# The output projection of a hybrid decoder block: seven block products for eight, and the low parts of its weights made by DMA

## The chip, the cores and the metric

The kernel runs on one core of one Trainium2 chip. The metric is the device time of one execution in microseconds; of the kernel before there are three timed runs and one execution under the profiler. Times in the text that name no run are microseconds from the start of the profiled span.

## The reference

One layer of a hybrid block on x of 2048 tokens by 1024 channels, all in float32. An input projection feeds a pooling mixer (512 channels) and a gated DeltaNet (4 heads of 128), their results are put side by side, and an output projection with a residual and a last norm ends it:

```python
n = rms_norm(h, norm_w[layer])
proj = jnp.einsum('bsd,de->bse', n, w_in[layer])
...
y_pool = pool_mixer(pu, pz, pool_w[layer], pool_scale[layer])
y_dn = deltanet_mixer(q, k, v, dz, b, a, conv_w[layer], a_log[layer],
                      dt_bias[layer], dn_norm_w[layer])
y = jnp.concatenate([y_pool, y_dn], axis=-1)
h = h + jnp.einsum('bse,ed->bsd', y, w_out[layer])
return rms_norm(h, final_norm_w)
```

The change is in the last two lines: y (2048 x 1024) times w_out (1024 x 1024), plus x, then the norm of each row.

## The kernel before

TensorE multiplies in a rounded 32-bit format (fp32r). To keep float32's precision each operand is written as a high part (rounded to fp32r) and a low part (the rest), and each product of two operands is made of three matmuls: high by high, high by low, low by high. All of them are 128x128 weights against 512 columns.

The kernel walks the sequence in two blocks of 1024 tokens, and in each through the input projection (L375 to L377), whose results feed the convolutions, the pooling and the DeltaNet chain of each head. The branches' results go to a DRAM buffer, y_dram, in 16 tiles of 128 tokens (L405, by SP's queue). After the last projection comes the output stage, on which this document turns:

- W_out is held in two halves of 512 columns, nh (high) and nl (low), in the buffers which the normalised input of the last block had (two of each, so the first half can come as soon as the first half block's projections have ended, the second when the last has). load_wo (L838) fetches raw pieces of 512 KB by SP's queue into four buffers of the DeltaNet part, split_wo (L842) copies them to nh on ScalarE (L847) and subtracts for nl on VectorE (L178).
- Each tile of y is loaded into wh by GpSimd's queue (load_y, L858), and its low part made in wl by split_y: ScalarE writes minus the high part (L865) and a DMA from GpSimd's queue adds y to it on the way (L866, accum_op=add: an accumulating DMA). wh and wl have three buffers each, which the weights of the input projection had before.
- out_mm (L868) makes for a tile, a half of the columns and one of eight slices of 128 channels the three matmuls L872, L873 and L874. A tile's half is eight slices, 24 matmuls; in the text a slot is one slice, three matmuls. The stage has 16 tiles, 256 slots, 768 matmuls.
- out_add (L876) adds the residual on VectorE (L881) and sums the squares on ScalarE (L883); out_norm (L885) makes 1/sqrt by 13 small steps on VectorE (L888, L889 and rsqrt, L168 to L175), scales (L895) and stores (L898, SP's queue).

TensorE's order is the order in which the events are traced: at(slot, function) gives each step its slot, and the steps are sorted by it. On the other engines a scheduler sets the order when the kernel is built; each engine and each DMA queue then takes its instructions strictly in that order. Two queues issue the kernel's DMAs: SP's (plain transfers) and GpSimd's (POOL; plain and accumulating).

Of the kernel before, what the change touches and what calls it, by code (L numbers as in the profile page):

```python
# [19 lines left out]
NB = SEQ // TB  # L20
HALF = 512
# [24 lines left out]
    (("dec", 4), ("dec", 4), ("dec", 4), ("kdec", 2)),  # L46
    (("dec", 4), ("kdec", 2), ("kT", 2), ("kT", 2)),
)
WO_TAGS = ("At", "Ai", "Tt", "kT")

E_PU, E_PZ, E_Q, E_K, E_V, E_Z = 0, 4, 8, 12, 16, 20

# [25 lines left out]
def hymba_kernel(  # L78
# [18 lines left out]
    nc = tc.nc  # L97
# [9 lines left out]
    def st(shape, dt, tag, bufs=1):  # L107
        return sp.tile(shape, dt, tag=tag, name=tag, bufs=bufs)
# [68 lines left out]
    def split_lo(eng, lo, full, hi):  # L177
        eng.tensor_tensor(out=lo, in0=full, in1=hi, op=ALU.subtract)  # L178
# [163 lines left out]
    events = []  # L342
# [1 line left out]
    free.update({(t, i): -99 for t in ("kdec", "kT", "qT", "sz") for i in range(2)})  # L344

    def at(slot, fn, *args):
        events.append((slot, len(events), fn, args))

    def load_w(w, et, first):
        w["hi"] = st([P, KT, P], F32R, "wh", 3)  # L350
# [384 lines left out]
    slot = 0  # L735
# [3 lines left out]
    for b in range(NB):  # L739
# [13 lines left out]
        i = 0  # L753
# [79 lines left out]
        for h, res in heads:  # L833
            delta(b, h, res, gt, ends[h], ready)

    wo = {"hi": {}, "lo": {}}
# [5 lines left out]
    def split_wo(i, hf):  # L842
# [4 lines left out]
        nc.scalar.copy(wo["hi"][hf][:, ks], wo["raw", i, hf])  # L847
        split_lo(nc.vector, wo["lo"][hf][:, ks], wo["raw", i, hf], wo["hi"][hf][:, ks])

    def load_fw():  # L850
        wo["fw"] = fw = st([P, D], F32, "v0")
        nc.gpsimd.dma_start(fw, final_w[None, :].to_broadcast([P, D]))

    def load_y(ti, o):
        o["y"] = y_dram[ti]
        o["hi"] = st([P, KT, P], F32R, "wh", 3)
        o["lo"] = st([P, KT, P], F32R, "wl", 3)
        nc.gpsimd.dma_start(o["hi"], o["y"])  # L858

    def load_res(ti, o):  # L860
        o["x"] = xr = st([P, D], F32, "kdec", 2)
        nc.sync.dma_start(xr, x[ti * P : (ti + 1) * P, :])

    def split_y(o):
        nc.scalar.activation(o["lo"], o["hi"].bitcast(F32), AF.Copy, scale=-1.0)  # L865
        nc.gpsimd.dma_start(o["lo"], o["y"], accum_op=ALU.add)  # L866

    def out_mm(o, hf, k):  # L868
        if k == 0:
# [3 lines left out]
        nc.tensor.matmul(ps, o["hi"][:, k], wo["lo"][hf][:, k], start=False, stop=False)  # L873
        nc.tensor.matmul(ps, o["lo"][:, k], wo["hi"][hf][:, k], start=False, stop=(k == KT - 1))  # L874

    def out_add(o, hf):  # L876
        if hf == 0:
            o["h"] = st([P, D], F32, "dec", 4)
            o["s2"] = st([P, 2], F32, "s2o", 2)
        dsl = slice(hf * HALF, (hf + 1) * HALF)  # L880
        nc.vector.tensor_tensor(out=o["h"][:, dsl], in0=o["ps", hf], in1=o["x"][:, dsl], op=ALU.add)  # L881
        junk = st([P, HALF], F32, "acc", 3)
        nc.scalar.activation(junk, o["h"][:, dsl], AF.Square, accum_out=o["s2"][:, hf : hf + 1])  # L883

    def out_norm(ti, o):  # L885
        ht, s2 = o["h"], o["s2"]
        v = st([P, 1], F32, "vo", 2)
        nc.vector.tensor_tensor(out=v, in0=s2[:, 0:1], in1=s2[:, 1:2], op=ALU.add)  # L888
        nc.vector.tensor_scalar(out=v, in0=v, scalar1=1.0 / D, scalar2=EPS, op0=ALU.mult, op1=ALU.add)  # L889
        r = st([P, 1], F32, "ro", 2)  # L890
        rsqrt(r, v, [P, 1])
        step = HALF if ti == SEQ // P - 1 else D
        for o0 in range(0, D, step):
            cs = slice(o0, o0 + step)
            nc.vector.scalar_tensor_tensor(  # L895
                out=ht[:, cs], in0=ht[:, cs], scalar=r[:, 0:1], in1=wo["fw"][:, cs], op0=ALU.mult, op1=ALU.mult
            )
            nc.sync.dma_start(out[ti * P : (ti + 1) * P, cs], ht[:, cs])  # L898
# [7 lines left out]
    order = []  # L906
    for i in range(0, SEQ // P, 2):
        if i == 0:
            order += [(i, 0), (i + 1, 0), (i, 1), (i + 1, 1)]
        else:  # L910
            order += [(i, 0), (i, 1), (i + 1, 0), (i + 1, 1)]
    for ti, hf in order:
        o = outs[ti]
        if hf == 0:
            at(slot - 30, load_y, ti, o)
            at(slot - 20, load_res, ti, o)
            at(slot - 20, split_y, o)
        for k in range(KT):
            at(slot + k, out_mm, o, hf, k)
        slot += KT  # L920
        at(slot, out_add, o, hf)
        if hf == 1:
            at(slot + 1, out_norm, ti, o)

    with tc.manual_schedule(engines={mybir.EngineType.PE}):
        for _, _, fn, args in sorted(events, key=lambda e: e[:2]):
            fn(*args)


def layout(inputs):  # L930
# [42 lines left out]
```

## Time and profile before

| what | value |
|---|---|
| three timed runs | 1006.75, 1006.88, 1007.75 us (median 1006.88) |
| the profiled execution | 1006.09 us, of it the span 1004.4 us |
| mean granted TensorE clock | 0.994 |
| busy in the window 900 to 950 us (all output stage) | TensorE 50.00 of 50.00, VectorE 22.11, ScalarE 11.84 |
| the same window's DMA share and rate | 0.71, 199 GB/s |
| first matmul of the output stage | 820.5 us |

A row of a timeline gives the start, the duration, the engine, the line and operation, and in brackets how long the engine stood idle before it and what ended that. Matmuls overlap: each is shown with 0.39 us, and they start 0.2267 us apart. A row of a table by windows gives the window, its length, the busy time and count of each engine (PE, weight loads, VectorE, ScalarE, GpSimd), the granted clock, the DMA share (mean busy share of the 16 DMA engines) and GB/s. For a DMA instruction the duration is that of its issue, not of the transfer.

### The profile page before, as it was taken

How to read it: one execution, taken by the hardware profiler on the slowest of the kernel's cores; microseconds unless marked ns; L12 is line 12 of the kernel's file. 1: busy time of each engine (PE TensorE's matmuls, PEld its weight loads, DVE VectorE, ACT ScalarE, POOL GpSimd, SP SyncE). 2: the span in 40 equal slices, each digit the busy share in tenths (PEclk: the TensorE clock that was granted, in tenths of full speed). 3: DMA queues.
4: the chain of work that ended last, by engine and by line, in shares of the span. 5: the costliest groups of instructions: out<-in, count | busy, mean ns of one | idle time of the engine just before them, and what ended most of it. 6: DMA issues, size and time to landing. Idle time of an engine off the chain costs nothing.

```text
span 1004.4 us, 14802 instructions
## 1 busy us (share of the span) xinstructions
PE 950.2 (95%) x5252; PEld 757.1 (75%) x5252; DVE 652.3 (65%) x2032; ACT 485.4 (48%) x1205; POOL 147.6 (15%) x200
## 2 busy tenths in 40 slices
PE   4989999989999999999899999999999999999996
PEld 3667777778777787767677777777778778888885
DVE  6676978668588355957886866858835483443343
ACT  7357665565564435516855455556443332222211
POOL 2214200101000014104410010101001101111100
PEclk9999999999999999999999999999999999999999
DMA  7431333332424346424242242242444576777761
GB/s 252 90 84 43 75 78 58 77 82 45 112 64 113 78 105 163 101 58 106 57 91 42 62 92 60 48 89 63 103 108 106 151 195 178 193 206 195 185 185 63
DMA packets 49434, 106.90 MB, mean 106 GB/s; under 512 B 4688, under 2 KB 22352, under 8 KB 49360
## 3 DMA queue, kind: packets, MB, share of 16 engines
q0 software_dynamic: 18000, 65.54, 30.4%
q1 hardware_dynamic: 31360, 40.41, 12.1%
q8 instruction: 41, 0.67, 0.3%
q14 instruction: 33, 0.27, 0.1%
HBM read 89.16 MB, written 16.78 MB: 105 GB/s over the span
## 4 chain that ended last, share of the span: by engine, by line
PE 56%; DVE 6%; issue 6%; DMA 4%; ACT 4%; POOL 0%; DVEq 0%; ACTq 0%; POOLq 0%
PE ps L375 10%; PE ps L377 9%; PE ps L376 9%; PE pso L874 6%; PE pso L873 6%; PE pso L872 6%; DMA wh<-in_w_in_dram 3%; PE ch L631 1%; PE tp L465 1%; DVE Ai L511 1%; PE qp L532 1%; PE ch L653 1%; PE ob L641 1%; PE ch L647 1%; PE ob L657 1%
## 5 line engine op out<-in xcount | busy, mean ns | idle before, releaser
L375 PE MATMUL ps<-nh,wh 128*128 128x512 f32 x768 | 335.6, 437 | 10.6 <-ACT nh L193 10.6
L377 PE MATMUL ps<-nh,wl 128*128 128x512 f32 x768 | 303.0, 395 | 1.8 <-DMA wl<-in_w_in_dram 1.8
L376 PE MATMUL ps<-nl,wh 128*128 128x512 f32 x768 | 302.3, 394 | 2.3 <-DVE nl L194 2.3
L375 PEld LDWEIGHTS ps<-nh,wh 128*128 128x128 f32 x768 | 145.9, 190 | 36.9 <-ACT nh L193 11.2
L377 PEld LDWEIGHTS ps<-nh,wl 128*128 128x128 f32 x768 | 145.0, 189 | 34.9 <-DMA wl<-in_w_in_dram 2.7
L376 PEld LDWEIGHTS ps<-nl,wh 128*128 128x128 f32 x768 | 146.1, 190 | 27.7 <-DVE nl L194 4.4
L389 DVE SCALAR_TENSOR_TENSOR acc<-u,cw,acc 128x512 f32<-128x512 f32 x144 | 112.5, 781 | 10.7 <-ACT acc L387 9.1
L872 PE MATMUL pso<-nh,wh 128*128 128x512 f32 x256 | 100.0, 391 | 0.0
L874 PE MATMUL pso<-nh,wl 128*128 128x512 f32 x256 | 99.7, 389 | 0.2 <-DMA wl<-y_dram 0.2
L873 PE MATMUL pso<-nl,wh 128*128 128x512 f32 x256 | 99.6, 389 | 0.0
L358 POOL DMA_DIRECT2D wh<-in_w_in_dram x46 | 26.6, 579 | 388.1 <-PE ps L377 375.0
L881 DVE TENSOR_TENSOR dec<-pso,kdec 128x512 f32<-128x512 f32 x32 | 22.1, 691 | 80.1 <-PE pso L874 80.1
L384 DVE TENSOR_TENSOR u<-ps,rb 128x512 f32<-128x512 f32 x48 | 33.1, 689 | 57.5 <-PE ps L377 57.3
L366 ACT ACTIVATE wl<-wh 128x1024 fp32r<-128x1024 f32 x46 | 48.8, 1061 | 44.0 <-DMA wh<-in_w_in_dram 35.2
L367 POOL DMA_DIRECT2D wl<-in_w_in_dram x46 | 39.7, 863 | 184.9 <-ACT wl L366 93.4
L883 ACT ACTIVATE acc<-dec 128x512 f32<-128x512 f32 x32 | 20.1, 629 | 85.3 <-DVE dec L881 85.3
L387 ACT ACTIVATE acc<-u,cw 128x512 f32<-128x512 f32 x48 | 34.6, 721 | 54.5 <-DVE u L384 52.4
L548 DVE TENSOR_TENSOR tmp<-Ai,X 128x60 f32<-128x60 f32 (+24 forms) x248 | 53.5, 216 | 4.0
L874 PEld LDWEIGHTS pso<-nh,wl 128*128 128x128 f32 x256 | 48.1, 188 | 10.6 <-DMA wl<-y_dram 0.6
L872 PEld LDWEIGHTS pso<-nh,wh 128*128 128x128 f32 x256 | 48.1, 188 | 10.2 <-ACT nh L847 0.2
L873 PEld LDWEIGHTS pso<-nl,wh 128*128 128x128 f32 x256 | 48.1, 188 | 10.0 <-issue 0.2
L554 DVE TENSOR_TENSOR X<-X,tmp 128x60 f32<-128x60 f32 (+24 forms) x248 | 52.5, 212 | 4.5
(214 smaller groups left out, 1511.4 us busy)
## 6 DMA issues: line engine op xcount, KB each, us to landing
wh<-in_w_in_dram POOLq DMA_DIRECT2D x46, 512.0 KB, 3.8
wl<-in_w_in_dram POOLq DMA_DIRECT2D x46, 512.0 KB, 5.6
y_dram<-yt SPq DMA_DIRECT2D x32, 256.0 KB, 3.1
kdec<-in_x_dram SPq DMA_DIRECT2D x16, 512.0 KB, 4.5
wh<-y_dram POOLq DMA_DIRECT2D x16, 512.0 KB, 4.0
wl<-y_dram POOLq DMA_DIRECT2D x16, 512.0 KB, 6.4
out_dram<-dec SPq DMA_DIRECT2D x15, 512.0 KB, 2.7
dec<-in_xT_dram SPq DMA_DIRECT2D x7, 512.0 KB, 7.8
```

The source lines that it names most:

```text
L366: nc.scalar.activation(w["lo"], w["hi"].bitcast(F32), AF.Copy, scale=-1.0)
L367: nc.gpsimd.dma_start(w["lo"], w_in[et], accum_op=ALU.add)
L375: nc.tensor.matmul(ps, w["hi"][:, k], nh[:, k], start=(k == 0), stop=False)
L376: nc.tensor.matmul(ps, w["hi"][:, k], nl[:, k], start=False, stop=False)
L377: nc.tensor.matmul(ps, w["lo"][:, k], nh[:, k], start=False, stop=(k == KT - 1))
L387: nc.scalar.activation(acc, ub[:, HALO:], AF.Copy, scale=cw[:, ci, CONV - 1 : CONV])
L389: nc.vector.scalar_tensor_tensor(out=acc, in0=ub[:, h0 + j : h0 + j + HALF], scalar=cw[:, ci, j : j + 1], in1=acc, op0=ALU.mult, op1=ALU.add,)
L548: nc.vector.tensor_tensor(out=tmp[:, 0:n, 0:w], in0=Ai[:, j, j + 1 : BS].unsqueeze(1).to_broadcast([P, n, w]), in1=X[:, 0:n, j : j + 1].to ...
L554: nc.vector.tensor_tensor(out=X[:, 0:n, j + 1 : BS], in0=X[:, 0:n, j + 1 : BS], in1=tmp[:, 0:n, 0:w], op=ALU.subtract)
L872: nc.tensor.matmul(ps, o["hi"][:, k], wo["hi"][hf][:, k], start=(k == 0), stop=False)
L873: nc.tensor.matmul(ps, o["hi"][:, k], wo["lo"][hf][:, k], start=False, stop=False)
L874: nc.tensor.matmul(ps, o["lo"][:, k], wo["hi"][hf][:, k], start=False, stop=(k == KT - 1))
```

## The change

Tiles 0 to 3 are computed as before, though the right half of the columns (hf=1) goes ahead of the left. The other twelve are taken in six pairs. For a pair, the two tiles are the two block rows of a 2x2 block matrix A (columns: the two halves of the 1024 channels) and W_out is the 2x2 block matrix B. The four block results take eight block products, which a Strassen scheme (Winograd's form) makes of seven with sums of blocks. Each block product is four slots, so that a pair has 28 slots, 84 matmuls, in place of 96:

```diff
+    PRODUCTS = (
+        ("A", "A11", "B11", True),
+        ("C", "S1", "T1", True),
+        ("B", "A12", "B21", True),
+        ("A", "S2", "T2", False),
+        ("C", "S4", "B22", False),
+        ("D", "A22", "T4", True),
+        ("A", "S3", "T3", False),
+    )
```

A, B, C, D are PSUM banks. Bank A is read after its first product, accumulated on, read again, accumulated on again. The sums of W_out's blocks, T1 to T4, are made once, in the time of tiles 0 to 3, from pieces of W_out that SP's queue loads again as float32 (t_load). Each T is split into high (ScalarE copy) and low (ScalarE minus the high, then an accumulating DMA whose source is an SBUF tile):

```diff
+    def lower(lo, hi, src):
+        nc.scalar.activation(lo, hi.bitcast(F32), AF.Copy, scale=-1.0)
+        nc.gpsimd.dma_start(lo, src, accum_op=ALU.add)
...
     def load_wo(i, hf):
-        wo["raw", i, hf] = wr = st([P, 2, HALF], F32, *((t := WO_TAGS[(4 * hf + i) % len(WO_TAGS)]), 2 if t == "kT" else 1))
-        nc.sync.dma_start(wr, w_out[:, 2 * i : 2 * i + 2, hf * HALF : (hf + 1) * HALF])
...
+        nc.gpsimd.dma_start(wo["hi"][hf][:, 2 * i : 2 * i + 2], wo_src(i, hf))
+
+    def split_wo(i, hf):
         ks = slice(2 * i, 2 * i + 2)
-        nc.scalar.copy(wo["hi"][hf][:, ks], wo["raw", i, hf])
-        split_lo(nc.vector, wo["lo"][hf][:, ks], wo["raw", i, hf], wo["hi"][hf][:, ks])
+        lower(wo["lo"][hf][:, ks], wo["hi"][hf][:, ks], wo_src(i, hf))
+
+    def t_load(k, w):
+        w["bd"] = bd = st([P, 2, HALF], F32, "yr1", 2)
+        nc.sync.dma_start(bd, w_out[:, k : KT : NP, half(1)])
+        w["a"], w["c"] = st([P, HALF], F32, "u", 3), st([P, HALF], F32, "acc" if k == 3 else "rb", 3)
+        nc.sync.dma_start(w["a"], w_out[:, k, half(0)])
+        nc.sync.dma_start(w["c"], w_out[:, k + NP, half(0)])
+
+    def t_sums(k, w):
+        a, b, c, d = w["a"], w["bd"][:, 0], w["c"], w["bd"][:, 1]
+        minus = lambda o, x0, x1: nc.vector.tensor_tensor(out=o, in0=x0, in1=x1, op=ALU.subtract)
...
+    def t_split(k, w, name):
...
+        nc.scalar.copy(hi, w[name])
+        lower(lo, hi, w[name])
```

A pair's y comes by SP's queue as float32 (pair_load) and is summed and split on VectorE and ScalarE (pair_a, pair_b, pair_c: 5 casts of 512 columns and one of 1024 on ScalarE, 4 sums, 5 subtractions of 512 and one of 1024 on VectorE). The residual comes in by an accumulating DMA onto a copy of a PSUM bank, four of 256 KB for each pair:

```diff
+    def pair_seed(q, bank, o, ti, hf):
+        if "h" not in o:
+            o["h"] = st([P, D], F32, "dec", 4)
+        nc.scalar.copy(o["h"][:, half(hf)], q[bank])
+        nc.gpsimd.dma_start(o["h"][:, half(hf)], x[ti * P : (ti + 1) * P, half(hf)], accum_op=ALU.add)
```

Each pair's two norms are made together, with the 13 steps for both tiles at once; only those of the last pair apart, the second after the last add. Most steps of the stage on the other engines are "paced": they get an order dependency, without a semaphore, on the matmul traced last before them, so that the scheduler does not put them ahead of it:

```diff
+            for ins in new:
+                if held and ins.engine != mybir.EngineType.PE:
+                    tc.add_manual_dep(ins, last.name, no_sync, reason="paced")
...
-            at(slot - 22 + 16 * hf + 0.1 * i, load_wo, i, hf)
-            at(slot - 14 + 15 * hf + 3 * i, split_wo, i, hf)
+            paced(slot - 16 + 15.5 * hf + 0.1 * i, load_wo, i, 1 - hf)
+            paced(slot - 12 + 15 * hf + 2 * i, split_wo, i, 1 - hf)
+    for k in range(NP):
+        w = {}
+        paced(slot + 6 + 6 * k, t_load, k, w)
+        ts = slot + 14 + 6 * k
+        paced(ts, t_sums, k, w)
+        paced(ts + 0.1, t_split, k, w, "T2")
+        paced(ts + 0.2, t_split, k, w, "T1")
+        paced(ts + 0.3, t_split, k, w, "T3")
+        paced(slot + 45 + 2 * k, t_split, k, w, "T4")
...
+        paced(slot - 32, pair_load, t, q)
+        paced(slot - 14, pair_a, q)
+        paced(slot - 10, pair_b, q)
+        paced(slot - 3, pair_c, q)
...
+        paced(done[0], pair_seed, q, "A", o1, t, 0)
+        paced(done[1], pair_seed, q, "C", o2, t + 1, 1)
+        paced(done[3], pair_seed, q, "A", o1, t, 1)
+        paced(done[5], pair_seed, q, "D", o2, t + 1, 0)
```

Nothing ahead of the output stage changes on TensorE. GpSimd's queue at the start of the stage, before (wh and wl are tiles of y from y_dram, high and low; v0 is the final norm's weight):

```order
L858 DMA wh_8147<-y_dram_93 128x1024
L367 DMA wl_7980<-in_w_in_dram 128x1024
L866 DMA wl_8148<-y_dram_93 128x1024
L852 DMA v0_8280<-in_final_norm_w_dram 128x1024
L858 DMA wh_8212<-y_dram_93 128x1024
L866 DMA wl_8213<-y_dram_93 128x1024
L858 DMA wh_8353<-y_dram_93 128x1024
L866 DMA wl_8354<-y_dram_93 128x1024
```

The same place now (nh and nl are the halves of W_out, high and low; line 864 is the accumulating DMA of lower, for y and W_out alike):

```order
L912 DMA wh_8147<-y_dram_93 128x1024
L387 DMA wl_7980<-in_w_in_dram 128x1024
L907 DMA v0_8276<-in_final_norm_w_dram 128x1024
L864 DMA wl_8148<-y_dram_93 128x1024
L873 DMA nh_8239<-in_w_out_dram 128x2x512 x4
L864 DMA nl_8240<-in_w_out_dram 128x2x512
L912 DMA wh_8210<-y_dram_93 128x1024
L864 DMA nl_8240<-in_w_out_dram 128x2x512 x3
L873 DMA nh_8324<-in_w_out_dram 128x2x512 x4
L864 DMA wl_8211<-y_dram_93 128x1024
L912 DMA wh_8344<-y_dram_93 128x1024
L864 DMA nl_8325<-in_w_out_dram 128x2x512 x4
```

Between the tiles of y stand now sixteen transfers of W_out, eight of them accumulating; the low part of the second tile (wl_8211) stands behind the second half's four high parts.

Further down the same queue, where before only wh and wl of the next tiles follow in turn (tiles 3 and 4, and the high part of tile 5), before:

```order
L858 DMA wh_8431<-y_dram_93 128x1024
L866 DMA wl_8432<-y_dram_93 128x1024
L858 DMA wh_8532<-y_dram_93 128x1024
L866 DMA wl_8533<-y_dram_93 128x1024
L858 DMA wh_8616<-y_dram_93 128x1024
```

and now (qT, Tt and sz hold the low parts of T1, T3 and T2; wh_8395 and wl_8396 are tile 3):

```order
L864 DMA qT_8430<-u_8367 128x512
L864 DMA wl_8345<-y_dram_93 128x1024
L864 DMA Tt_8435<-yr1_8365 128x512
L864 DMA sz_8425<-yr1_8365 128x512
L864 DMA qT_8430<-u_8403 128x512
L864 DMA Tt_8435<-yr1_8401 128x512
L864 DMA sz_8425<-yr1_8401 128x512
L912 DMA wh_8395<-y_dram_93 128x1024
L864 DMA wl_8396<-y_dram_93 128x1024
```

Five accumulating transfers of 256 KB stand between the low part of tile 2 and tile 3, a sixth ahead of both.

SP's queue around the start of the stage, before:

```order
L405 DMA y_dram_93<-yt_8174 128x4x128
L840 DMA At_8311<-in_w_out_dram 128x2x512
L840 DMA Ai_8313<-in_w_out_dram 128x2x512
L840 DMA Tt_8315<-in_w_out_dram 128x2x512
L405 DMA y_dram_93<-yt_8262 128x4x128
L405 DMA y_dram_93<-yt_8361 128x4x128
L862 DMA kdec_8403<-in_x_dram 128x1024
```

and now (yr1, u, rb and acc are the pieces of W_out for the T sums, dec the residual):

```order
L425 DMA y_dram_93<-yt_8174 128x4x128
L916 DMA dec_8264<-in_x_dram 128x1024
L425 DMA y_dram_93<-yt_8256 128x4x128
L881 DMA yr1_8365<-in_w_out_dram 128x2x512
L883 DMA u_8367<-in_w_out_dram 128x512
L884 DMA rb_8368<-in_w_out_dram 128x512
L425 DMA y_dram_93<-yt_8354 128x4x128
L881 DMA yr1_8401<-in_w_out_dram 128x2x512
L883 DMA u_8403<-in_w_out_dram 128x512
L884 DMA rb_8404<-in_w_out_dram 128x512
L916 DMA dec_8410<-in_x_dram 128x1024
L883 DMA u_8455<-in_w_out_dram 128x512
```

The loads for the T sums stand on this queue from just before the stage's start on.

More of the change, by code (lines that the diff above doesn't have):

```diff
@@ L885, in out_norm @@
[L885 to L888, printed above, removed]
-        nc.vector.tensor_scalar(out=v, in0=v, scalar1=1.0 / D, scalar2=EPS, op0=ALU.mult, op1=ALU.add)
[L890 to L898, printed above, removed]
+        nc.vector.tensor_tensor(out=o["h"][:, half(hf)], in0=ps, in1=src[:, half(hf)], op=ALU.add)
@@ new lines, in pair_sums, with pair_load, pair_split @@
+    def pair_sums(t):
+        sq = st([P, 2, 2], F32, "s2o", 2)
+        for j in range(2):
+            outs[t + j]["sq"], outs[t + j]["s2"] = sq, sq[:, j]
+    def pair_load(t, q):
+        q["r1"] = st([P, KT, P], F32, "yr1", 2)
+        nc.sync.dma_start(q["r1"], y_dram[t])
+        for name, tag, lo in (("r21", "ps_s", 0), ("r22", "sacc", NP)):
+            q[name] = st([P, NP, P], F32, tag, 2)
+            nc.sync.dma_start(q[name], y_dram[t + 1][:, lo : lo + NP])
+    def pair_split(hi, lo, raw):
+        nc.scalar.copy(hi, raw)
+        split_lo(nc.vector, lo, raw, hi)
@@ new lines, in pair_mm @@
+    def pair_mm(q, bank, a, b, fresh, k):
+        if fresh and k == 0:
+            pool, tag = BANKS[bank]
+            q[bank] = pool.tile([P, HALF], F32, tag=tag, name="ps" + bank)
+        ps = q[bank]
+        (ah, al), (bh, bl) = (t[:, k] for t in q[a]), w_part(b, k)
+        args = dict(skip_group_check=True)
+        nc.tensor.matmul(ps, ah, bh, start=(fresh and k == 0), stop=False, **args)
+        nc.tensor.matmul(ps, ah, bl, start=False, stop=False, **args)
+        nc.tensor.matmul(ps, al, bh, start=False, stop=(k == NP - 1), **args)
@@ L904, in hymba_kernel @@
     at(slot - 10, load_fw)
     outs = [{} for _ in range(SEQ // P)]
[L906 to L912, printed above, removed]
-        o = outs[ti]
[L914 to L917, printed above, removed]
+    for ti, hf in ((0, 1), (1, 1), (0, 0), (1, 0), (2, 1), (3, 1), (2, 0), (3, 0)):
+        o = outs[ti]
+        if hf == 1:
+            paced(slot - 30, load_y, ti, o)
+            paced(slot - 20, load_res, ti, o)
+            paced(slot - 20, split_y, ti, o)
+            if ti % 2 == 0:
+                at(slot, pair_sums, ti)
```

141 lines of the change are left out of this document (119 added, 22 removed).

## The prediction, on record before the changed kernel was run

> **What bounds the kernel now.** I read the page first, for the engines' shares and the slices. They say that TensorE is full to the end and that the DMA engines are busiest in the last fifth:
>
> ```profile
> PE 950.2 (95%) x5252; PEld 757.1 (75%) x5252; DVE 652.3 (65%) x2032; ACT 485.4 (48%) x1205; POOL 147.6 (15%) x200
> DMA  7431333332424346424242242242444576777761
> ```
>
> Then TensorE's waits from 740 us to the end, two in all, 0.9 us together:
>
> ```profile
> PE ps L377 <- DMA wl<-in_w_in_dram: 0.7, 1, 0.7
> PE pso L874 <- DMA wl<-y_dram: 0.2, 1, 0.2
> ```
>
> So the output stage is bound by the number of its matmuls. Their spacing and the stage's ends come from TensorE's timeline (two rows 21 matmuls apart, the last matmul, the first step behind it) and from the group of line 872:
>
> ```profile
> 900.05 0.39 PE L872 MATMUL pso<-nh,wh 128*128 128x512 f32 x1
> ...
> 904.81 0.39 PE L872 MATMUL pso<-nh,wh 128*128 128x512 f32 x1
> ...
> 995.70 0.39 PE L874 MATMUL pso<-nh,wl 128*128 128x512 f32 x1
> 996.13 0.69 DVE L881 TENSOR_TENSOR dec<-pso,kdec 128x512 f32<-128x512 f32 x1 [4.75 <-PE pso L874]
> ```
>
> ```profile
> L872 PE MATMUL pso<-nh,wh x256: 389/389/798, 820.5 to 995.2; 128*128 128x512 f32 x128
> ```
>
> (904.81 - 900.05)/21 = 0.2267 us for a matmul, 0.68 us for a slot. The stage starts at 820.5, its last matmul at 995.7. From the first step behind TensorE (996.13) to the end of the span (1004.4) it is 8.3 us, and the profiled execution's 1006.1 us hold 1.7 us beside the span. The median of the timed runs is 0.8 us above that execution, under the 0.2% (2 us) that a measurement of this kernel can tell from no change; I forecast for the profiled execution and let the median stand at the same place.
>
> **What the seven products save.** The order of the changed kernel shows 84 matmuls for each of six pairs where 96 were: 72 x 0.2267 = 16.3 us, all on TensorE and so all on the path, if TensorE stays fed.
>
> **What a transfer costs.** The change moves W_out's low parts from VectorE to accumulating DMAs. VectorE's subtractions (row of 1.22 us below, eight) hid beside TensorE, which waited for none of them, so removing them gains nothing. The price of the DMAs is in windows in which one transfer ran nearly alone (a fetch of 512 KB issued at 625.14, an accumulate of 512 KB at 630.36), in one that holds the four transfers of a tile (wl, wh, residual, result), and in the kernel's last store:
>
> ```profile
> 625.14 0.56 POOL L358 DMA_DIRECT2D wh<-in_w_in_dram  x1 [12.13 <-PE ps L377]
> 630.36 0.85 POOL L367 DMA_DIRECT2D wl<-in_w_in_dram  x1 [4.66 <-ACT sqj L472]
> ```
>
> ```profile
> 626.00:629.00 3.00, 1.22 (x7) 0.93 (x7) 2.96 (x13) 1.56 (x5) 0.00 (x0) 1.00 0.55 178
> 631.00:636.00 5.00, 5.00 (x31) 4.39 (x30) 4.29 (x20) 2.02 (x9) 0.21 (x1) 1.00 0.67 105
> 855.00:864.00 9.00, 9.00 (x41) 7.46 (x40) 4.29 (x16) 1.97 (x4) 0.68 (x2) 1.00 0.81 235
> ```
>
> ```profile
> q1 hardware_dynamic: 288, 0.52, 14.1%
> ```
>
> The last two columns of a window are DMA share and GB/s. Alone, a fetch keeps all 16 engines for 3 x 0.55 = 1.65 us, an accumulate for 5 x 0.67 = 3.35 us. The last 0.52 MB (queue row of the window 995 to 1005) take 14.1% of 10 us, 1.41. The tile's four take 9 x 0.81 = 7.3 us, so an accumulate among others costs 7.3 - 3 x 1.41 = 3.1. I take 1.4 for a plain unit of 512 KB and 3.1 for an accumulating one, since the change runs them close together as that window does; the lone prices are the upper end. The Trainium skill ("DMA: Bandwidth & Descriptors", "Anatomy of one DMA — SWDGE (gpsimd) path") prices a transfer at about 2.0 us plus bytes over 436 GB/s and sets nothing apart for adding; by that a unit of either kind would move in 1.2 us, an estimate from that page, and the sum below would end at 1002.2, faster. The trace's 3.35 us for a lone accumulate speaks against it.
>
> Transfers of GpSimd's queue finish in its order. Issued 0.56 us apart, the accumulate ends TensorE's wait at 827.61 and the fetch behind it ends ScalarE's at 828.82, 6.2 us after its issue:
>
> ```profile
> 822.08 0.88 POOL L866 DMA_DIRECT2D wl<-y_dram  x1 [6.23 <-ACT wl L865]
> 822.64 0.89 POOL L858 DMA_DIRECT2D wh<-y_dram  x1
> 827.61 0.50 PE L874 MATMUL pso<-nh,wl 128*128 128x512 f32 x1 [0.16 <-DMA wl<-y_dram]
> 828.82 1.06 ACT L865 ACTIVATE wl<-wh 128x1024 fp32r<-128x1024 f32 x1 [2.73 <-DMA wh<-y_dram]
> ```
>
> **The walk through the queue.** W_out's first half can't be fetched before the last block's first half leaves nh. The trace has that moment, where ScalarE's first copy was let go, and the one at which tile 1's buffer came free:
>
> ```profile
> 808.93 1.05 ACT L847 CAST nh<-At 128x1024 fp32r<-128x1024 f32 x1 [8.17 <-PE ps L377]
> 815.30 0.55 POOL L858 DMA_DIRECT2D wh<-y_dram  x1 [12.81 <-PE ps L377]
> ```
>
> First bytes move some 0.9 us after an issue (625.14 to 626), so the walk starts at 809.8. I add the transfers in the new order, those of SP's queue put where they become ready, as work for the same engines, in units of 512 KB (a half is 256 KB), and compare with TensorE's due times: slot s at 820.5 + 0.68 s.
>
> 1. To the last low part of W_out's first half: one residual, 4 fetches of nh, the fetch of tile 1, SP's y store, yr1, u and rb (2.5 units), in all 8.5 plain, 11.9; and 4 accumulates, 12.4. End 834.1. Due in slot 6 at its second matmul, 824.8: TensorE is 9.3 late.
> 2. Tile 1's low part stands behind four more fetches: 4 + 5 units of SP's queue (yr1 and a residual, 2; a y store and five halves, 3) = 9 plain, 12.6; one accumulate, 3.1. End 849.8. Due in slot 8 at its third matmul, 826.4 + 9.3 = 835.7: 14.1 more, 23.4 in all.
> 3. The second half's low parts: one fetch, four accumulates, 13.8. End 863.6; due in slot 22, 835.7 + 23.4 = 859.1: 4.5 more, 27.9.
> 4. Tile 3: six low parts of T (halves, 9.3), tile 2's low part 3.1, tile 3's fetch 1.4, SP's three halves 2.1: 879.5. Then ScalarE's copy, the issue and 0.9 us to the first byte, 2.0 together, and the accumulate: 884.6. Due in slot 40, 848.2 + 27.9 = 876.1: 8.5 more, **36.4 us** of stalls.
>
> Ends without the accumulates' price: all at 1.4, the walk gives 2.5 + 12.4 = 14.9; at the lone prices 12.4 + 16.6 + 5.8 + 10.4 = 45.2.
>
> **The pairs themselves.** Prices for VectorE and ScalarE, from the stage's groups by form:
>
> ```profile
> L881 DVE TENSOR_TENSOR dec<-pso,kdec 128x512 f32<-128x512 f32 x32 | 22.1, 691 | 80.1 <-PE pso L874 80.1
> L895 DVE SCALAR_TENSOR_TENSOR dec<-dec,ro,v 128x1024 f32<-128x1024 f32 x15 | 19.3, 1284 | 0.5
> L178 DVE TENSOR_TENSOR nl<-At,nh 128x1024 fp32r<-128x1024 f32 x2 | 2.4, 1221 | 1.4 <-ACT nh L847 1.4
> L883 ACT ACTIVATE acc<-dec 128x512 f32<-128x512 f32 x32 | 20.1, 629 | 85.3 <-DVE dec L881 85.3
> ```
>
> A pair lasts 84 x 0.2267 = 19.0 us. VectorE has 13 steps of 512 columns (9.0), one split of 1024 (1.2), two scalings (2.6) and the norm's 13 small steps, at some 0.2 each 2.6: 15.4. ScalarE has 13 of 512 (8.2), one of 1024 and small reads: 10. The DMA engines have 4 plain units and four seeds of a half unit, 5.6 + 6.2 = 11.8. None reaches 19.0, so I cost the pairs' sums, splits and seeds at nothing. Cover gone, VectorE is the first that would cost, at what it exceeds 19.0 by, six times. The pacing adds order, no semaphore.
>
> **The tail.** Bank D ends 12 matmuls, 2.7 us, before the last; its copy (0.63), GpSimd's issue with 0.9 us to the first byte, 1.55 of transfer and some 0.5 for the semaphores end about 1 us after TensorE, where before the add started at once; with a store ahead on the engines it is 3. I take 2.0.
>
> **The sum.** 1006.1 - 16.3 + 36.4 + 2.0 = 1028.2; I forecast **1028 us**. Plain prices in the walk would make it 1006.7, lone ones 1037.0.
>
> **Rivals.**
>
> The accumulates cost no more than fetches. Four in a row hide each other's start, which a lone one, or one among fetches, can't show. The walk at 1.4 leaves 14.9 of stall, 1006.7 us. Against it stands the window of the tile, where one accumulate among three plain transfers still took 3.1. By the Trainium skill ("DMA: Bandwidth & Descriptors", "Two DMAs through the same engine are not ordered") descriptors of one queue start in order but are pipelined, which would help this rival; no run shown so far has two accumulates in a row. Chance 0.13.
>
> Faster: transfers overlap so far that a unit of either kind costs 1.0. Then only step 2 stalls: 822.3 after step 1, 832.3 against 826.4, 5.9 us, and the kernel takes 1006.1 - 16.3 + 5.9 + 2.0 = 997.7. It decides where the stall falls below 16.3 - 2.0 = 14.3, at about 1.37 a unit; the fastest row is 1.41, plain. Chance 0.10.
>
> Slower still: the pairs don't hold their pace. The add of bank B waits for seed A's DMA, and behind it on VectorE stand the next pair's sum and its split of A11 and A12, due at slot 28. The seed is asked for at slot 4 and lands some 4 us later, slot 10; the add may start as late as slot 24. Only if seeds land over 9.5 us late does a pair stretch; at 3 us each, 1028 + 18 = 1046. Chance 0.05.
>
> That the change doesn't do what it says: the order shows 72 matmuls fewer. Chance 0.02 for any surprise of that kind.
>
> **How the numbers follow.** The forecast's case has 0.70. Of the first rival's 0.13 I put 0.03 on faster, 0.03 within 0.2%, 0.07 on slower. Faster 0.13, same 0.03, slower 0.84. The range reaches from 1003, which takes in the first rival and leaves out most of the second, to 1042, above the lone prices' 1037 for what the walk left out; some 0.15 lies outside.
>
> **What would show it.** Right, if TensorE's waits of the changed kernel name DMAs of nl and wl between 820 and 890, with the longest at tile 1's low part, and the first product of the first pair starts near 864 + 36 = 900 in place of 864; if the DMA share there is near 1; if from then on the pairs run at 19.0 us without a wait. Wrong, if two accumulates in a row land less than 2 us apart, if the waits name VectorE or ScalarE, or if the first pair starts before 878, where the stall no longer eats the saving.

## The result, and the profile after

The changed kernel takes 1033.49 us (median of 4, 1030.26 to 1035.00), the kernel before beside it 1007.32 (1006.75 to 1007.75): a ratio of 1.0256, interval 1.0231 to 1.0281. The forecast was 1028. The profiled execution of the changed kernel took 1035.0 us, of it 1033.3 the span.

The page first, by its engines, its slices and the queue that the change lengthens (packets, MB, share of 16 engines):

```profile
PE 947.1 (92%) x5180; PEld 751.5 (73%) x5180; DVE 679.8 (66%) x2010; ACT 525.9 (51%) x1285; POOL 179.5 (17%) x232
...
PE   5998999989999999999999999999999857699995
...
DMA  7431323323334346433332241422333999956644
...
q0 software_dynamic: 24656, 71.84, 33.4%
```

TensorE has 72 instructions fewer and yet the program is longer. Where its row was full to the end, it dips to 5 in the last fifth, in the very slices in which the DMA row stands at 9. VectorE and ScalarE have more to do than before, and neither is full. TensorE's waits from 740 us to the end (us in total, times, the longest):

```profile
PE pso L927 <- DMA wl<-y_dram: 17.1, 2, 8.6
PE pso L926 <- DMA nl<-in_w_out_dram: 11.4, 6, 5.4
PE pso L925 <- DMA wh<-y_dram: 2.6, 1, 2.6
```

31.1 us in all, where it was 0.9, and every one ends with a DMA. The first rows of pso and psA (first and last start are the two times behind the counts) and the last matmul bound the stages:

```profile
L925 PE MATMUL pso<-nh,wh x64: 387/389/798, 821.5 to 905.0; 128*128 128x512 f32 x64
```

```profile
L1022 PE MATMUL psA<-nh,wh x24: 389/389/393, 905.7 to 1003.3; 128*128 128x512 f32 x24
...
1020.12 0.40 PE L1024 MATMUL psA<-Ai,wl 128*128 128x512 f32 x1
```

The stage starts at 821.5 (820.5 before). Its 64 slots of single tiles need 43.5 us undisturbed, so the first pair was due at 865.0; it comes 40.7 late. The waits make 31.1 of that; most of the rest are matmuls at half rate behind the three longest waits, some 6 us (below). The six pairs then take 114.4 us, 19.1 each. By windows:

```profile
820.00:830.00 10.00, 4.58 (x15) 3.03 (x13) 1.38 (x2) 3.52 (x4) 6.88 (x9) 0.70 1.12 288
830.00:840.00 10.00, 6.28 (x22) 3.71 (x21) 3.01 (x5) 2.57 (x5) 2.36 (x3) 0.96 1.18 305
840.00:850.00 10.00, 3.39 (x8) 2.71 (x9) 1.11 (x2) 5.30 (x8) 4.76 (x6) 0.55 1.10 280
...
880.00:890.00 10.00, 2.60 (x6) 2.11 (x7) 4.30 (x7) 5.62 (x12) 3.60 (x5) 0.50 1.05 238
...
925.00:1020.00 95.00, 95.00 (x419) 78.40 (x418) 63.84 (x138) 40.25 (x86) 16.16 (x19) 1.00 0.59 144
```

In the four windows shown up to 890 the DMA share is over 1 (it adds up what the packets of both queues took, so it can pass 1) and TensorE works 2.6 to 6.3 of each 10 us; in the three left out, 850 to 880, the share is 0.98 to 1.11 and TensorE works 6.2 to 8.5. In the pairs the share is 0.59 and TensorE works 95.00 of 95.00 us. So most of the loss lies in the stage's start, nothing is given back or lost in the pairs, and a smaller part comes behind the last matmul, in the tail: 13.2 us to the end of the span where it was 8.7.

### The profile page after: what moved, and what is told of

The parts are those of the page before. It is cut to its first block, busy times and chain, and to the rows that moved or that the text cites. A ratio compares the mean times of both kernels' runs of the same rounds, so it can differ in the third digit from the quotient of the medians.

```text
span 1033.3 us, 14842 instructions
## 1 busy us (share of the span) xinstructions
PE 947.1 (92%) x5180; PEld 751.5 (73%) x5180; DVE 679.8 (66%) x2010; ACT 525.9 (51%) x1285; POOL 179.5 (17%) x232
## 3 DMA queue, kind: packets, MB, share of 16 engines
q1 hardware_dynamic: 32432, 40.41, 11.9%
## 4 chain that ended last, share of the span: by engine, by line
PE 48%; issue 10%; DMA 7%; DVE 6%; ACT 4%; POOL 2%; DVEq 0%; POOLq 0%; ACTq 0%
PE ps L395 10%; PE ps L397 10%; PE ps L396 10%; DMA wh<-in_w_in_dram 2%; DMA nl<-in_w_out_dram 2%; DMA nh<-in_w_out_dram 1%; PE ch L651 1%; PE ch L673 1%; PE tp L485 1%; DVE Ai L531 1%; PE qp L552 1%; PE ob L661 1%; PE ch L667 1%; PE ob L677 1%; PE pm L458 1%
## 5 line engine op out<-in xcount | busy, mean ns | idle before, releaser
L934 ACT ACTIVATE t<-dec 128x512 f32<-128x512 f32 x32 | 20.2, 631 | 55.0 <-DVE dec L932 55.0
L927 PE MATMUL pso<-nh,wl 128*128 128x512 f32 x64 | 27.7, 433 | 17.1 <-DMA wl<-y_dram 17.1
L492 ACT ACTIVATE sqj<-tp 128x128 f32<-128x128 f32 x128 | 34.0, 277 | 16.3 <-PE tp L485 16.2
L680 ACT ACTIVATE sqj<-v 128x128 f32<-128x128 f32 x64 | 19.6, 306 | 38.1 <-DVE v L678 32.2
L1030 POOL DMA_DIRECT2D dec<-in_x_dram x24 | 20.4, 873 | 104.9 <-ACT dec L1029 58.7
L926 PE MATMUL pso<-nl,wh 128*128 128x512 f32 x64 | 27.7, 433 | 11.4 <-DMA nl<-in_w_out_dram 11.4
L651 PEld LDWEIGHTS ch<-state,kT 128*128 128x128 f32 x128 | 21.4, 188 | 21.6 <-DVE state L674 19.0
L669 ACT ACTIVATE nv<-ch,sm 128x128 f32<-128x128 f32 x64 | 23.4, 366 | 23.5 <-PE ch L667 23.4
## 6 DMA issues: line engine op xcount, KB each, us to landing
nl<-in_w_out_dram POOLq DMA_DIRECT2D x8, 512.0 KB, 13.3
```

The lines of the kernel that those rows point to most:

```text
L492: nc.scalar.activation(junk, tp[:, j], AF.Square, accum_out=dst[:, c : c + 1])
L651: nc.tensor.matmul(ch[:, 0], res["kT"][:, t], S, start=True, stop=True)
```

## The experiments

My theory: W_out's low parts by accumulating DMA fill GpSimd's queue and the DMA engines so far that tiles 0 to 3 wait for their operands. The main rival: the low parts of the T sums do it. Later rivals were the queue's order, the bytes of the transfers, and TensorE's own recovery after a wait. Ten kernels ran; ratios are against the kernel before on the same chip (medians there 1009.33, 1009.19 and 1007.47), and "late" is how long after its undisturbed time, 43.5 us behind the stage's first matmul, the first pair began in the profile.

| kernel | median us | ratio, interval | late | span after the last matmul's start |
|---|---|---|---|---|
| the change | 1033.49 | 1.0256, 1.0231 to 1.0281 | 40.7 | 13.2 |
| W_out's lows on VectorE | 1011.8 | 1.0015, 0.9995 to 1.0035 | 15.8 | 13.2 |
| T's lows on VectorE | 1031.32 | 1.0217, 1.0180 to 1.0253 | 32.9 | 13.6 |
| both on VectorE | 1005.92 | 0.9974, 0.9954 to 0.9994 | 10.9 | 13.0 |
| before, W_out's lows by DMA | 1028.88 | 1.0199, 1.0158 to 1.0240 | | |
| both, another order | 1004.56 | 0.9953, 0.9927 to 0.9980 | 8.2 | 12.8 |
| both, another tail | 1003.52 | 0.9950, 0.9933 to 0.9967 | 14.4 | 9.9 |
| both, order and tail | 999.34 | 0.9899, 0.9878 to 0.9919 | 8.7 | 9.9 |
| busy in the waits | 1034.58 | 1.0265, 1.0238 to 1.0293 | 37.8 | 13.5 |
| second half later | 1037.9 | 1.0308, 1.0239 to 1.0376 | 41.6 | 13.3 |
| W_out's lows by plain DMA | 1020.68 | 1.0128, 1.0074 to 1.0182 | 29.1 | 13.4 |

"Both" and "both, another tail" have the same start of the stage and are 3.5 us apart in the column "late": so far two profiled executions scatter there, and the ratios carry the verdicts. The column also leaves out when the stage itself began, 818.7 to 825.2 in these profiles.

### Who makes the low parts: W_out's, T's, both

W_out's own lows on VectorE again, the raw pieces by SP's queue, asked for at the slots of the kernel before and not paced:

```diff
-        lower(wo["lo"][hf][:, ks], wo["hi"][hf][:, ks], wo_src(i, hf))
+        nc.scalar.copy(wo["hi"][hf][:, ks], wo["raw", i, hf])
+        split_lo(nc.vector, wo["lo"][hf][:, ks], wo["raw", i, hf], wo["hi"][hf][:, ks])
```

> The changed kernel with W_out's own low parts as before (raw pieces by SP's queue, copy on ScalarE, subtraction on VectorE); the T sums keep their accumulating DMAs. Theory (the stall is the DMA engines' backlog, and W_out's eight fetches and eight accumulates on GpSimd's queue are most of it): TensorE's waits before the first pair fall from 31 us to some 13, the longest being tile 3's low part behind the T accumulates (about 6), and the time comes to 1005 to 1011 us. Rival (the T sums are the cause: their loads and their sixteen accumulates): the waits stay above 25 us and the time above 1022.

T's lows on VectorE, in t_split:

```diff
-        lower(lo, hi, w[name])
+        split_lo(nc.vector, lo, w[name], hi)
```

> The changed kernel with the low parts of T1 to T4 subtracted on VectorE in place of sixteen accumulating DMAs of 256 KB; W_out's own low parts stay by DMA. Theory (backlog, mostly W_out's): the waits up to tile 1 stay as they are, only tile 3's shrinks, and the time falls by 5 to 9 us, to 1024 to 1029. Rival (the T sums are the cause): 1010 or less.

Both edits:

> Both together: no low part of a weight by DMA, the seven products and the pacing kept. Theory: what is left of the wait is tile 1's and tile 3's low part, some 4 to 8 us with the slow matmuls behind them; saving 16.3, tail 4.5 longer: 997 to 1002 us, faster than both kernels. Rival (the seven products or the pacing cost time by themselves): 1008 or more, with waits inside the pairs.

TensorE's waits from 740 us on, of the three in this order (here and below rows of up to 1.3 us are left out where the text does not turn on them):

```profile
PE pso L932 <- DMA wl<-y_dram: 7.2, 2, 4.5
PE pso L930 <- DVE dec L937: 3.5, 1, 3.5
```

```profile
PE pso L927 <- DMA wl<-y_dram: 10.9, 2, 6.3
PE pso L926 <- DMA nl<-in_w_out_dram: 10.6, 5, 4.3
```

```profile
PE pso L932 <- DMA wl<-y_dram: 6.8, 2, 3.6
```

The row of nl is there whenever W_out's lows come by DMA, and gone when they don't. The two prices add up. W_out's lows, with the move of its fetches to GpSimd's queue, cost 1.0256 - 1.0015 = 0.0241 with T's by DMA and 1.0217 - 0.9974 = 0.0243 without: 24 us. T's cost 0.0039, which is no more than its interval, and 0.0041: 4 us, where I had expected 5 to 9. The rival falls. The wait of 3.5 us on VectorE (L937, an addition of the residual) in the first kernel I had not foreseen. The third kernel came out less fast than I had expected: seven products save 16.3 us, and 10.9 of lateness in the stage's start (of it 6.8 of waits on low parts of y) and 4.3 of a longer tail (13.0 for 8.7) eat nearly all of it.

### W_out's low parts by DMA in the kernel before

The same edit alone, with eight products and no T sums:

```diff
-        nc.scalar.copy(wo["hi"][hf][:, ks], wo["raw", i, hf])
-        split_lo(nc.vector, wo["lo"][hf][:, ks], wo["raw", i, hf], wo["hi"][hf][:, ks])
+        nc.scalar.activation(lo, hi.bitcast(F32), AF.Copy, scale=-1.0)
+        nc.gpsimd.dma_start(lo, w_out[:, ks, hf * HALF : (hf + 1) * HALF], accum_op=ALU.add)
```

> The kernel before with one part of the change alone: W_out's high parts fetched by GpSimd's queue and its low parts by accumulating DMAs, at the change's slots; eight products, no T sums. Theory (backlog): waits of some 20 us in the first four half tiles, named by DMAs of nl and wl, and 1022 to 1034 us. Rival (the T sums and SP's loads make the backlog, W_out's low parts alone fit): within 4 us of the kernel before.

```profile
PE pso L874 <- DMA wl<-y_dram: 8.1, 1, 8.1
PE pso L873 <- DMA nl<-in_w_out_dram: 5.8, 4, 2.1
```

Slower by 20 us with nothing else of the change in it, and with the same two operands waited for (13.9 us in these rows, where I had expected some 20). The cause is not the Strassen scheme.

### The adding or the bytes

The eight transfers stay where they are, with the same bytes, but don't add:

```diff
-        lower(wo["lo"][hf][:, ks], wo["hi"][hf][:, ks], wo_src(i, hf))
+        nc.scalar.activation(lo, hi.bitcast(F32), AF.Copy, scale=-1.0)
+        nc.gpsimd.dma_start(lo, wo_src(i, hf))
```

> The changed kernel with the eight transfers that make W_out's low parts as plain ones of the same bytes from the same source, on the same queue in the same place; the low parts then hold W_out itself, so what is left out is the adding. Theory (an accumulating transfer of 512 KB costs 3.1 us of the queue where a plain one costs 1.4): 8 x 1.7 = 13.6 us less, 1018 to 1022 us, the waits on nl nearly gone, those on wl of tiles 1 and 3 still there. Rival (the bytes cost, not the adding): 1031 to 1035 us, no change.

TensorE's waits on wl and nl, and the page's row of these issues (KB, us to landing; 13.3 us in the change):

```profile
PE pso L929 <- DMA wl<-y_dram: 10.9, 2, 8.1
PE pso L928 <- DMA nl<-in_w_out_dram: 5.8, 4, 2.4
```

```profile
nl<-in_w_out_dram POOLq DMA_DIRECT2D x8, 512.0 KB, 8.6
```

0.0128 of the ratio, 12.9 us, is gone: 1.6 us for each of eight, near the 1.7 between the prices 3.1 and 1.4 (interval of the difference about 0.006 either way, 0.75 us each). The bytes alone are not it; the adding costs about as much again as a plain transfer of 1.4. It makes about half of the 24 us of W_out's lows. The other 11 us go with eight transfers more and with the fetches' move from SP's queue to GpSimd's; no run takes these two apart. The waits on nl are halved, not nearly gone, and one of 3.1 us on the high part of a tile of y stands beside them (2.6 in the change). The Trainium skill ("DMA: Bandwidth & Descriptors", "Anatomy of one DMA — SWDGE (gpsimd) path") prices a transfer by a fixed part and its bytes and sets nothing apart for adding; by that this kernel would have been as slow as the change, and the measurement decides against it.

### Order alone

The second half's fetches are asked for 3.5 slots later, so that tile 1's low part stands ahead of them (the expectations count a wait from start to start of two matmuls, 0.4 us longer than a bracket shows):

```diff
-            paced(slot - 16 + 15.5 * hf + 0.1 * i, load_wo, i, 1 - hf)
+            paced(slot - 16 + (19 if hf else 0) + 0.1 * i, load_wo, i, 1 - hf)
```

> The changed kernel with the same transfers in another order: the fetches of W_out's second half are asked for 3.5 slots later, so that the low part of y's tile 1 stands ahead of them in GpSimd's queue, not behind them. Theory (the stage's start is short of transfer time as a whole, so order only moves the waits): the wait of 8.9 us on tile 1's low part falls to 4 or 5, the waits on W_out's second half grow from 5 to some 15, and the first pair comes 0 to 4 us later than the change's 905.7: 1033 to 1038 us. Rival (the queue's order alone is at fault: one transfer stands behind four that are not needed yet): 1024 to 1026 us, with the other waits as they were.

GpSimd's queue and TensorE's waits:

```profile
831.17 0.89 POOL L864 DMA_DIRECT2D wl<-y_dram  x1 [5.63 <-ACT wl L863]
...
832.51 2.95 POOL L873 DMA_DIRECT2D nh<-in_w_out_dram  x4
```

```profile
PE pso L926 <- DMA nl<-in_w_out_dram: 24.1, 5, 14.0
PE pso L927 <- DMA wl<-y_dram: 3.5, 1, 3.5
```

Tile 1's low part now goes first and its wait is gone (I had expected 4 or 5 us of it to stay); the 3.5 us left, of 17.1, are on tile 3's. The waits on W_out rise from 11.4 to 24.1. The time doesn't fall. Order only moved the wait: the DMA share is 1.10 to 1.15 in every 10 us from 810 to 870, so the stage's start is short of transfer time as a whole.

### TensorE kept busy in the waits

In the change's trace the matmuls behind a long wait come at half their rate. Here is the one on tile 1's low part, up to the return to the usual spacing:

```profile
846.61 0.79 PE L927 MATMUL pso<-nh,wl 128*128 128x512 f32 x1 [8.51 <-DMA wl<-y_dram]
847.20 0.63 PE L925 MATMUL pso<-nh,wh 128*128 128x512 f32 x1
847.63 0.63 PE L926 MATMUL pso<-nl,wh 128*128 128x512 f32 x1
...
851.04 0.50 PE L925 MATMUL pso<-nh,wh 128*128 128x512 f32 x1
851.38 0.39 PE L926 MATMUL pso<-nl,wh 128*128 128x512 f32 x1
```

847.63 - 847.20 = 0.43 us from start to start where 0.2267 is usual, and the granted clock in 840 to 850 is 0.55 (windows above). Matmuls whose result nothing reads were put into the three long waits:

```diff
+    def warm(n):
+        junk = pd.tile([P, HALF], F32, tag="pd", name="warm")
+        for _ in range(n):
+            nc.tensor.matmul(junk, outs[0]["hi"][:, 0], wo["hi"][1][:, 0], start=True, stop=True)
+
+    WARM = {(0, 1): 22, (1, 1): 34, (3, 1): 44}
```

> The changed kernel with matmuls that compute nothing put ahead of three of its long waits at the stage's start (22 ahead of tile 0's second-order product of the second half, 34 ahead of tile 1's low part, 44 ahead of tile 3's), into a bank that nothing reads: about 5, 8 and 10 us of work where TensorE idled 5.8, 8.9 and 9.0 us. Theory (the eleven or twelve matmuls at 0.43 us instead of 0.227 behind each long wait come from TensorE's having stood idle): the slow ones vanish, 5 to 7 us less than the change, 1026.5 to 1028.5 us. Rival (they are slow for what the transfers do to memory, or the waits' ends move with them since the transfers set the pace): the slow ones stay, 1032 to 1035 us. If the added work is longer than a wait, it costs what it exceeds it by, 1 us or less each.

The three windows with the long waits, clock in the third column from the end, and the first matmuls of tile 3 behind the added ones:

```profile
820.00:830.00 10.00, 7.42 (x31) 5.48 (x31) 0.00 (x0) 2.15 (x3) 5.78 (x8) 1.00 1.13 243
840.00:850.00 10.00, 8.82 (x38) 6.62 (x36) 1.28 (x2) 5.13 (x8) 3.73 (x4) 1.00 1.09 285
880.00:890.00 10.00, 10.00 (x46) 8.26 (x44) 2.19 (x4) 8.00 (x16) 6.51 (x9) 1.00 1.09 198
```

```profile
883.88 0.39 PE L936 MATMUL pso<-nh,wh 128*128 128x512 f32 x1
884.10 0.39 PE L939 MATMUL pso<-nl,wh 128*128 128x512 f32 x1
```

The clock is 1.00 where it was 0.70, 0.55 and 0.50, and the spacing 0.22: the slow matmuls behind these three waits do come from TensorE's standing idle. Elsewhere in the same trace nine slow matmuls came all the same, from 858.18 to 862.53 (the clock in 850 to 860 is 0.78), behind two waits on nl of 2.4 and 2.1 us close together:

```profile
PE pso L939 <- DMA nl<-in_w_out_dram: 8.9, 6, 2.4
```

```profile
858.18 0.79 PE L939 MATMUL pso<-nl,wh 128*128 128x512 f32 x1 [2.09 <-DMA nl<-in_w_out_dram]
```

The Trainium skill ("TensorE: Matmul & The Clock Gate", "Part 1: The HAM clock gate (the "warmup" mystery)") says that an idle window of some 3.4 us puts the array at half its clock and a busy one of that length brings it back; the change's trace agrees in kind, with waits of 5.4, 8.5 and 8.6 us followed by 0.43 us of spacing and waits of up to 1.7 us that were not. In other runs the measurement goes against so plain a limit on a single wait: behind 3.15 us (both on VectorE, at 859.15) the spacing stayed as usual, and behind 2.67 us (W_out's lows on VectorE, at 833.30) it was 0.43 us for eight matmuls, from 1.5 us later on.

But the time did not fall: 1034.58 us, no change against the change. My 5 to 7 us were wrong, and the reason lies in the same trace: behind the first two waits TensorE runs into the next transfer, which lands when it lands. The waits on nl behind the first grew from 1.8 to 3.0 us, those behind the second from 4.2 to 5.4, and at slot 22 TensorE is as late as before (27.0 us for 26.4). Half-rate matmuls ahead of a later wait only shorten that wait. What counts is those behind the last one, from 887.40 to 905.7 in the change 18.3 us for 70 matmuls' 15.9: 2.4 us, too little for these runs to tell from none. The profiled execution shows that much (37.8 late for 40.7), and its four other runs took 1032.27 to 1036.72. No wait is left behind the last 44 added matmuls, so these may also have run past the landing.

### Towards a faster version

With all lows on VectorE, tile 2 takes both its halves before tile 3, and the T sums come 6 to 8 slots later:

```diff
-        paced(slot + 6 + 6 * k, t_load, k, w)
-        ts = slot + 14 + 6 * k
+        paced(slot + 12 + 6 * k, t_load, k, w)
+        ts = slot + 20 + 6 * k
...
-    for ti, hf in ((0, 1), (1, 1), (0, 0), (1, 0), (2, 1), (3, 1), (2, 0), (3, 0)):
+    for ti, hf in ((0, 1), (1, 1), (0, 0), (1, 0), (2, 1), (2, 0), (3, 1), (3, 0)):
```

> The change without any accumulating transfer for W_out and T (all their lows on VectorE again), and with the second half of the stage's start put in another order: tile 2 takes both its halves before tile 3, and the sums T1 to T4 are loaded and made 6 to 8 matmuls later. Same work as the version that has all lows on VectorE, which ran at 0.9974 of the kernel before with two waits on low parts of y, 6.8 us in all with 3.0 us of slow matmuls. Theory (the time at the stage's start is set by when the low parts of tiles 1 to 3 land in GpSimd's queue): tile 3's low part gets 8 more products of time, one wait of about 3 us is left, 3 us less than that version: ratio 0.994 to 0.995. Rival (the rest is set by the granted clock or by VectorE, not by this queue): no difference beyond 0.1%, ratio 0.997.

```profile
PE pso L930 <- DVE dec L937: 4.0, 1, 4.0
PE pso L932 <- DMA wl<-y_dram: 1.1, 1, 1.1
```

The waits on y fall from 6.8 to 1.1, as the theory has it. A wait of 4.0 takes their place that I had not seen: TensorE waits for a bank which VectorE has yet to read (L937, the addition of the residual). The ratio, 0.9953, lies just above what I expected; its interval takes in the rival's 0.997.

The last pair's residual loaded early by SP's queue, added on VectorE, and its additions asked for earlier (those of banks B and C half a slot behind their products instead of four, the last right behind the one before it):

```diff
     def pair_seed(q, bank, o, ti, hf):
+        if ti >= SEQ // P - 2:
+            nc.vector.tensor_tensor(out=o["h"][:, half(hf)], in0=q[bank], in1=o["h"][:, half(hf)], op=ALU.add)
+            return
```

> The same version with all lows on VectorE, and the last pair changed: its residual rows of x are loaded early by SP into the output tile and added on VectorE, where ScalarE's copy and the accumulating transfer that lands after the last matmul stood. Theory (the tail of 13.2 us after the last matmul of the change, where the kernel before had 8.7, is made of that transfer and the two additions behind it on VectorE): from the last matmul to the end 11 to 12 us, 1 to 2 us less in all, ratio 0.995 to 0.9965. Rival (the normalization of the last tile sets the tail whatever comes ahead of it): the tail stays at 13 us, ratio 0.9974.

Its tail, by the last matmul, the last two additions and the last scaling:

```profile
996.35 0.40 PE L1029 MATMUL psA<-Ai,wl 128*128 128x512 f32 x1
...
997.10 1.28 DVE L937 TENSOR_TENSOR dec<-psA,dec 128x512 f32<-128x512 f32 x2
...
1001.69 1.42 DVE L956 SCALAR_TENSOR_TENSOR dec<-dec,ro,v 128x512 f32<-128x512 f32 x2
```

From the last matmul to the end 9.9 us for 13.0: 3.1 less, more than I had expected; no run takes the residual's way and the earlier additions apart. Ratio 0.9950 against 0.9974, with intervals that overlap.

Both edits together:

> Both of these edits together: all lows of W_out and T on VectorE, tile 2's two halves before tile 3's, sums later, the last pair's residual loaded early. If their savings add as the theory has it, 4 to 5 us less than the version with all lows on VectorE: ratio 0.992 to 0.9935 of the kernel before, about 1000 to 1001 us where that one is 1008. If only one of them saves, 0.994 to 0.9965; if neither, 0.9974.

```profile
PE pso L930 <- DVE dec L937: 3.4, 1, 3.4
PE pso L932 <- DMA wl<-y_dram: 1.2, 1, 1.2
```

999.34 us, a ratio of 0.9899, 0.9878 to 0.9919: by the ratios it is 10 us faster than the kernel before and 36 faster than the change. Together the two edits save 0.0075 of the ratio where alone they saved 0.0021 and 0.0024: at least their sum, and more than I had expected (0.992 to 0.9935). Why more, the runs don't show. What is left at the stage's start is 8.7 us of lateness, of which 3.4 hang on VectorE.

## Why the prediction was right, point by point

**The direction and the place.** The time (1033.49) is within the range and 5.5 us above the forecast. What the text named as the sign of being right is in the trace: the waits name DMAs of nl and wl between 820 and 890, the two longest (8.5 and 8.6 us) are on the low parts of tiles 1 and 3, the DMA share is 0.98 to 1.18 there, and the pairs run without a wait. Three details were off: the longest is tile 3's by 0.1 us and not tile 1's, one wait of 2.6 is on a high part of y, and the first pair starts at 905.7 for "near 900".

**The saving.** 72 matmuls are gone and the pairs take 19.1 us each for 19.0. Their casts, sums and seeds were costed at nothing, and cost nothing.

**The price of an accumulate.** It was set at 3.1 us among others, 1.7 above a plain transfer. The low parts of W_out landed one after another, seen where TensorE took up work again:

```profile
831.07 0.50 PE L926 MATMUL pso<-nl,wh 128*128 128x512 f32 x1 [0.86 <-DMA nl<-in_w_out_dram]
...
836.19 0.50 PE L926 MATMUL pso<-nl,wh 128*128 128x512 f32 x1 [0.94 <-DMA nl<-in_w_out_dram]
...
856.89 0.50 PE L926 MATMUL pso<-nl,wh 128*128 128x512 f32 x1 [1.23 <-DMA nl<-in_w_out_dram]
860.25 0.50 PE L926 MATMUL pso<-nl,wh 128*128 128x512 f32 x1 [1.70 <-DMA nl<-in_w_out_dram]
863.11 0.50 PE L926 MATMUL pso<-nl,wh 128*128 128x512 f32 x1 [1.22 <-DMA nl<-in_w_out_dram]
```

Two in 5.1 us in the first half (TensorE did not visibly wait for the first of them), 3.4 and 2.9 us apart in the second, so not the less than 2 us that the text named as a sign of being wrong. But this sign does not decide: with plain transfers in their place TensorE took up work again at 845.97 and 848.84, 2.9 us apart as well. What fells the rival in which an accumulate costs no more than a fetch is the time of that kernel, 12.9 us less (1.6 each for the forecast's 1.7), and the one at 1.0 a unit falls with the 40.7 us of lateness where it had 5.9.

**The walk.** Each point of it is a matmul of the rows above; its due time is counted from the stage's own start, 821.5.

| step | predicted late | measured |
|---|---|---|
| 1, slot 6, at 836.19 | 9.3 | 10.4 |
| 2, slot 8, at 846.61 | 23.4 | 19.2 |
| 3, slot 22, at 863.11 | 27.9 | 26.4 |
| 4, slot 40, at 887.40 | 36.4 | 38.3 |
| the first pair, 905.7 | 36.4 | 40.7 |

The end of the walk is right within 2 us, in part by luck: step 2 was over-sized by 5.3, and steps 3 and 4 were under-sized by 2.7 and 3.4. Step 2 put five units of SP's queue whole ahead of tile 1's low part. The queues' rows (packets, MB, share of 16 engines) in the window from 836 to 846.5 say otherwise:

```profile
q0 software_dynamic: 1116, 2.63, 89.3%
q1 hardware_dynamic: 753, 0.72, 25.1%
```

SP's queue moved 0.72 MB there, 1.4 units; the window lies between the landing of the first half's last low part (836.19) and of tile 1's (846.61). So step 2 added 8.8 us where I had 14.1. What SP's queue did not get then it took later: 1.89 MB from 846.6 to 863.1, when nothing new was asked of it, and step 3 added 7.2 for 4.5. In step 4 the walk counted too little: from 863.1 to 887.4 SP's queue moved 3.41 MB, 6.5 units where the walk had 1.5, and tile 3's accumulate landed 8.0 us after its issue; the step added 11.9 for 8.5. One reading was short, too: in the trace of before, the lone fetch's first bytes move 1.1 us or a little more after its issue (no DMA from 625.80 to 626.20), not 0.9.

**Two terms that were missing or too small.** The matmuls at half rate behind the last wait were not in the sum: 40.7 against 38.3 at the pairs' start, 2.4 us. And the tail: forecast +2.0, measured 13.2 - 8.7 = 4.5. VectorE's rows show why:

```profile
1018.41 0.69 DVE L932 TENSOR_TENSOR dec<-psC,dec 128x512 f32<-128x512 f32 x1 [5.69 <-DMA dec<-in_x_dram]
1019.96 0.16 DVE L942 TENSOR_TENSOR vo<-s2o 128x1 f32<-128x1 f32 x1 [0.85 <-ACT t L934]
...
1022.27 1.42 DVE L951 SCALAR_TENSOR_TENSOR dec<-dec,ro,v 128x512 f32<-128x512 f32 x2
1023.60 0.68 DVE L932 TENSOR_TENSOR dec<-psA,dec 128x512 f32<-128x512 f32 x1
1024.68 0.69 DVE L932 TENSOR_TENSOR dec<-psA,dec 128x512 f32<-128x512 f32 x1 [0.39 <-DMA dec<-in_x_dram]
```

I had looked only at the last seed's transfer. The norm of the pair's first tile stands on VectorE from 1019.96 to 1023.6, ahead of an addition whose operand TensorE had finished by about 1020.5; the last transfer costs only the last 0.39 us behind that. The norm itself comes that late because the first tile's last addition waited until 1018.41 for the seed before. In the kernels with another tail 3.1 us went, with the last pair's seeds and copies gone and the additions put ahead.

Term by term for the profiled execution: 1006.1 - 16.3 + 40.7 + 4.5 = 1035.0, which is what it took; that the stage began 1.0 later is made up for by 1.1 that the stage of before took beyond its 768 matmuls' 174.1.

**What stays open.** Why adding about doubles a transfer's time is not settled; the runs show the price, not its mechanism. Nor do they take apart the 11 us of W_out's lows that are not the adding. Whether pacing cost anything by itself was not tried apart from the rest. Of the 10.9 us that the kernel with all lows on VectorE still loses at the start, 6.8 are waits on y, 2.8 are half-rate matmuls behind the first of them and 0.9 goes to two matmuls of the pooling part (L458) among the stage's; what makes those parts of y late was not followed further than by the run with another order.

## What to carry to other kernels

Moving work from an engine that isn't full to DMA is no gift when the stage's own loads go through the same engines: add up the transfers that must land before TensorE's next operand, in the queue's order, and price an accumulating one at about twice a plain one. Where such a sum overruns, changing the order may only move the wait, as it did here; take transfers away. Time that TensorE loses ahead of another wait for the same transfers cost nothing extra here, so look first at what lies behind the last wait, and at the tail.

## What the hardware showed that I had not expected

- Behind waits of 8.5 and 8.6 us 10 to 12 matmuls came 0.43 us apart, behind one of 5.4 us six of them, at a granted clock of 0.50 to 0.70 in the window, then 0.2267 again; with TensorE kept busy in the wait they came at 0.22 at once. Shorter waits went both ways: 3.15 us without slow matmuls behind it, 2.67 us with eight.
- Eight 512 KB transfers without the adding took 12.9 us less, 1.6 each, for the same bytes on the same queue.
- With both queues full, GpSimd's moved 2.63 MB and SP's 0.72 MB in the same 10.5 us, for 1116 packets against 753.
